# The causal mask of a block-sparse attention: from two TensorE matmuls a block to a VectorE add, with two query blocks sharing a pair of score banks

## The chip, the cores and the metric

The kernel runs on one core of a Trainium2 chip. The metric is the device time of one execution in microseconds. Lower is better. TensorE (PE) does the matmuls, VectorE (DVE), ScalarE (ACT) and GpSimd (POOL) the work on elements, and SyncE (SP) issues most transfers. Matmul results land in PSUM, which has eight banks of 512 fp32 values in each of 128 partitions; everything else lies in SBUF.

## The reference

Two decoder layers on a sequence of 512 tokens of width 1024. Each layer feeds three causal token mixers (a pooling, a short convolution, an attention) from one input projection, gates and adds their outputs, and then runs a gated feed-forward part. The change touches only the attention. It has 8 heads of 64 dimensions, and its sequence is cut into 2 blocks of 256 keys:

```python
gate = einsum('bhqd,bhnd->bhqn', q_i, kmean)        # queries against each block's mean key
gate = where(past, gate, NEG)                       # only blocks before the query's own
s_sel = where(valid, einsum(q_i, k_sel) * scale, NEG)
s_own = einsum('bhqd,bhkd->bhqk', q_i, k_own) * scale
s_own = where(kpos[None, :] <= qpos[:, None], s_own, NEG)    # the causal mask
p = softmax(concatenate([s_sel, s_own], axis=-1))
out = einsum(p_sel, v_sel) + einsum(p_own, v_own)
```

With two blocks only, the queries of the second block see the first block whole (the kernel has a penalty for the case in which the reference masks it) and their own block up to the diagonal.

## The kernel before

All activations lie transposed, features on the partitions. Every fp32 product is made of three matmuls on values split into a high part and a rest: high by high, high by rest, rest by high. The splits of the weights are made on the way: ScalarE copies the high part (`whi`, L327) and VectorE subtracts (`wlo`, L330). All matmuls go through one helper, L151, and all transposes through L157; both keep the program's order on TensorE. The order on the other engines is set by a scheduler when the program is built, except for instructions that are pinned.

**The order around the attention is written by hand.** The ordinary matmuls of the gates and of the branch projections run as the main line. Every 2,048 columns of main matmuls a *tick* happens. At a tick every *fiber* (a generator) that is due goes one step on; after that `run_bulk` adds `bulk_rate` to a credit and issues side tasks while the credit lasts. In layer 0 the side tasks of this stage are 16 long dot products of VectorE (L376, each of 1,024 elements, with a transfer of its own on the sync queue), which make two of the six modulation vectors. In layer 1 there are no side tasks in this stage. What is left of them is flushed after the attention projection (L954).

**The attention** (L661) is one fiber. For each of the 4 head pairs it makes the transposed queries and keys (`to_features`, four transposes each) and then starts four units, one for each block of 128 queries, with `GAP` = 2, 3, 3, 3 ticks between them. A unit (L580) has three steps:

1. It takes a pair of PSUM banks (`ps_pair`, of which two exist), one bank for each of the two heads. It writes the mask into the diagonal block of each bank by a matmul of a bf16 identity with a bf16 mask, and then accumulates six score matmuls on it, three for each head. A score matmul uses 64 rows of the array, since a head has 64 dimensions; the two heads use different rows. The score width is 256 columns for units 0 and 1, 384 for unit 2 and 512 for unit 3. VectorE then takes the maximum, ScalarE the exponentials with their sums, VectorE the reciprocal and the scaling (L598 to L623).
2. `WAIT` = 2, 3, 3, 3 ticks later TensorE transposes the probabilities (L157), ScalarE and VectorE split them (L634, L635).
3. Two ticks later TensorE multiplies them with the values (L644), and the result is put together and split (L649 to L654).

So unit 0's transposes fall on the tick at which unit 1 starts, unit 1's on the tick of unit 2, unit 2's on that of unit 3; unit 3's have a tick for themselves. Units 0 and 1 put the product of step 3 into a bank of its own, units 2 and 3 into the first of their score banks.

Of the kernel before, what the change touches and what calls it, by code (L numbers as in the profile page):

```python
# [12 lines left out]
F32 = mybir.dt.float32  # L13
F32R = mybir.dt.float32r
BF16 = mybir.dt.bfloat16
# [6 lines left out]
P = 128  # L22
# [5 lines left out]
HD = 64  # L28
PAIRS = HEADS // 2
TT = S // P  # L30
# [5 lines left out]
BLOCK = 256  # L36
# [43 lines left out]
def hybrid_trunk(ctx, tc, xT, ws, ada, cols, pool_w, qk_w, crow, pos, con, out):  # L80
    nc = tc.nc
    V, A, T = nc.vector, nc.scalar, nc.tensor

    const = ctx.enter_context(tc.tile_pool(name="const", bufs=1))
# [8 lines left out]
    def nm(s):  # L93
        uid[0] += 1
        return f"{s}{uid[0]}"

    def bigt(dt=F32R):
        return big.tile([P, S], dt, tag="big", name=nm("big"))

    def tmp():  # L100
        return work.tile([P, S], F32, tag="tmp", name=nm("tmp"), bufs=5)

    def ps_mm():
        return psum.tile([P, S], F32, tag="mm", name=nm("mm"), bufs=4)

    def ps_pair():
        return psum.tile([P, 2, S], F32, tag="pair", name=nm("pair"), bufs=2)

    def w4(shape, dt=F32):
        return work.tile(shape, dt, tag="w4", name=nm("w4"), bufs=6)  # L110

    def sm(shape, dt=F32, tag="sm", bufs=8):
        return small.tile(shape, dt, tag=tag, name=nm(tag), bufs=bufs)
# [8 lines left out]
    bulk_rate, credit = [0.0], [0.0]  # L122
# [27 lines left out]
    def matmul(*a, **k):  # L150
        tc.keep_in_program_order(T.matmul(*a, **k))  # L151
# [4 lines left out]
    def transpose(*a):  # L156
        tc.keep_in_program_order(T.transpose(*a))  # L157
# [38 lines left out]
    ident = const.tile([P, P], F32, name="ident")  # L196
    make_identity(nc, ident)
    ones = const.tile([P, P], F32, name="ones")
    nc.gpsimd.memset(ones, 1.0)
    ident16 = const.tile([P, P], BF16, name="ident16")  # L200
    nc.gpsimd.tensor_copy(ident16, ident)
    mask = const.tile([P, P], BF16, name="mask")
    nc.gpsimd.memset(mask, 0.0)
    nc.gpsimd.affine_select(out=mask, in_=mask, compare_op=ALU.is_ge, fill=NEG,
                            base=0, pattern=[[-1, P]], channel_multiplier=1)
# [207 lines left out]
    def ada_tasks(l, parts, early=False):  # L413
        out = []
        for part in parts:
            for j in range(KT):
                out.append((1.2, lambda part=part, j=j: ada_step(l, part, j, early)))
            out.append((0.2, lambda part=part: ada_end(l, part)))
        return out
# [157 lines left out]
    GAP = (2, 3, 3, 3)  # L577
    WAIT = (2, 3, 3, 3)

    def unit(hp, i, q, k, v, y, nrq, prq):  # L580

        w = P * (i + 1)
        wm = max(w, BLOCK)
        s = ps_pair()

        for a in range(2):
            matmul(s[:, a, i * P:w], ident16, mask, start=True, stop=True)
        for z, (qa, ka) in enumerate(((0, 0), (0, 1), (1, 0))):
            for a in range(2):
                r = slice(a * HD, (a + 1) * HD)  # L590
                matmul(s[:, a, :wm], q[qa][r, i * P:(i + 1) * P], k[ka][r, :wm],
                       start=False, stop=(z == 2), skip_group_check=True)
        cell = lambda: sm([P, 2], tag="asm", bufs=16)
        nsc, sc = nrq[:, i, 2 * hp:2 * hp + 2], prq[:, i, 2 * hp:2 * hp + 2]
        m, nb, den = cell(), cell(), cell()
        pr = [tmp() for _ in range(2)]
        if w <= BLOCK:
            V.tensor_reduce(m, s[:, :, :w], axis=AX.X, op=ALU.max)  # L598
            V.tensor_mul(nb, m, nsc)
            for a in range(2):  # L600
                A.activation(pr[a][:, :w], s[:, a, :w], AF.Exp, bias=nb[:, a:a + 1],
                             scale=sc[:, a:a + 1], accum_out=den[:, a:a + 1])
        else:

            gs, pen, mp, nbp, d2 = cell(), cell(), cell(), cell(), cell()
            V.tensor_reduce(gs, s[:, :, :BLOCK], axis=AX.X, op=ALU.add)
            V.tensor_mul(gs, gs, sc)
            V.tensor_scalar(pen, gs, NEG * BLOCK * SCALE, NEG, op0=ALU.is_lt, op1=ALU.mult)
            V.tensor_reduce(mp, s[:, :, :BLOCK], axis=AX.X, op=ALU.max)
            V.tensor_add(mp, mp, pen)  # L610
            V.tensor_reduce(m, s[:, :, BLOCK:w], axis=AX.X, op=ALU.max)
            V.tensor_max(m, m, mp)
            V.tensor_mul(nb, m, nsc)
            V.tensor_add(nbp, nb, pen)
            for a in range(2):
                A.activation(pr[a][:, :BLOCK], s[:, a, :BLOCK], AF.Exp, bias=nbp[:, a:a + 1],
                             scale=sc[:, a:a + 1], accum_out=den[:, a:a + 1])
                A.activation(pr[a][:, BLOCK:w], s[:, a, BLOCK:w], AF.Exp, bias=nb[:, a:a + 1],
                             scale=sc[:, a:a + 1], accum_out=d2[:, a:a + 1])
            V.tensor_add(den, den, d2)  # L620
        V.reciprocal(den, den)
        for a in range(2):
            V.tensor_scalar(pr[a][:, :w], pr[a][:, :w], den[:, a:a + 1], None, op0=ALU.mult)  # L623
        yield WAIT[i]

        pt = [None] * 2
        for aa in ([0, 1],) if i < 2 else ([0], [1]):
            n = len(aa)
            tp = ps_mm().rearrange("p (j a q) -> p j a q", a=n, q=P)[:, :i + 1]
            for a in aa:  # L630
                for j in range(i + 1):
                    transpose(tp[:, j, a - aa[0], :], pr[a][:, j * P:(j + 1) * P], ident)
            both = w4([P, i + 1, n, 2, P], F32R)
            A.activation(both[:, :, :, 0], tp, AF.Copy)  # L634
            V.tensor_sub(both[:, :, :, 1], tp, f32(both)[:, :, :, 0])  # L635
            for a in aa:
                pt[a] = both[:, :, a - aa[0]]
        yield 2


        po = (s[:, 0] if i >= 2 else ps_mm()).rearrange("p (a h q) -> p a h q", a=2, h=2)
        for a in range(2):
            for j in range(i + 1):
                matmul(po[:, a].rearrange("p h q -> p (h q)"), v[hp // 2][j][:, hp % 2 * 2 + a].rearrange("p h d -> p (h d)"),  # L644
                       pt[a][:, j].rearrange("p h q -> p (h q)"), start=(j == 0), stop=(j == i))
        c = slice(i * P, (i + 1) * P)
        t = tmp()
        part, total = t[:HD, :2 * P].rearrange("p (a q) -> p a q", a=2), t[:, 2 * P:3 * P]
        A.activation(part, po[HD:, :, 0], AF.Copy)  # L649
        V.tensor_add(part, part, po[:HD, :, 1])  # L650
        for a in range(2):
            V.tensor_add(total[a * HD:(a + 1) * HD], part[:, a], po[:HD, a, 0])
        A.activation(y[0][:, c], total, AF.Copy)
        V.tensor_sub(y[1][:, c], total, f32(y[0])[:, c])  # L654
# [6 lines left out]
    def attention(l, qk, v, nrq, prq, y_attn):  # L661

        for hp in range(PAIRS):
            q = to_features(l, qk, 0, hp)
            yield 1
            k = to_features(l, qk, 1, hp)
            y = bigt(), bigt()
            y_attn.append(y)
            yield 2
            for i in range(TT):  # L670
                start(unit(hp, i, q, k, v, y, nrq, prq))
                if i < TT - 1:
                    yield GAP[i]
            yield 1
# [45 lines left out]
    for l in range(L):  # L720
# [7 lines left out]
        for n, (k, lo, hi) in enumerate([(k, 0, S) for k in range(KT)] if l == 0 else HALVES + REST):  # L728
# [17 lines left out]
            w = held[k]  # L746
# [94 lines left out]
        for j in range(2):  # L841
# [8 lines left out]
            z = bigt(F32)  # L850
# [33 lines left out]
        for t in range(TT):  # L884
            for half in range(2):
                src = v_ps[t][:, half * BLOCK:(half + 1) * BLOCK].rearrange("p (n d) -> p n d", d=HD)
                o = v[half][t]
# [15 lines left out]

        if l == 0:
            bulk.extend(ada_tasks(l, (SC2, SH2), True))
        bulk_rate[0] = 0.35
        ahead_now[0] = 3

        def gate():
# [194 lines left out]
        for part, (along, single, pairs) in enumerate(PARTS):  # L1104
# [18 lines left out]
            for _ in range(single):  # L1123
                wg = next_w()
                g = ps_mm()
                feature_tile(g, wg)
                u = ps_mm()
# [5 lines left out]
            if l + 1 < L:  # L1133
                if part == 0:
                    later = ada_tasks(l + 1, (SC1, SH1, SC2, SH2))
                n = DOTS[part]
# [4 lines left out]
            if part + 1 < len(PARTS):  # L1141
                for n in range(KT):
                    if n == KT // 2:
                        bulk_rate[0] = 0.0
                    o = ps_mm()
# [117 lines left out]
```

## Time and profile before

| | us |
|---|---|
| time before, median of 3 runs | 1461.12 |
| lowest and highest of the 3 | 1460.99, 1461.18 |
| the profiled execution's own time | 1461.3 |
| its span in the profile | 1459.5 |
| TensorE matmuls busy | 1451.3 |
| VectorE busy | 1053.5 |
| ScalarE busy | 665.8 |
| GpSimd busy | 105.9 |

The profile is of one execution. The span goes from the first instruction to the last; the execution's own time has what lies around it too. TensorE's clock was granted in full throughout (1.00). Matmuls overlap in their pipeline, so the busy time of a group of matmuls is more than what it holds up; the distance from one matmul's start to the next one's is what it takes of TensorE's row. In the timeline, a row is "start us, us, engine line op out<-in xcount", and neighbouring instructions of one kind are merged.

### The profile page before, as it was taken

The page shows a single profiled execution, that of the slowest core. Times are in us where ns is not written, and L with a number is a line of the kernel's source. Part 1 is how long each engine was busy: PE and PEld are TensorE (multiplying, and loading weights), DVE is VectorE, ACT ScalarE, POOL GpSimd, SP SyncE. Part 2 cuts the span into 40 slices and gives each one's busy share as a digit, 9 for nine tenths or more (in the row PEclk, how much of TensorE's full clock was granted, in tenths as well). Part 3 has the DMA queues.
Part 4 walks back from the last instruction along what each step waited for, and adds up shares of the span by engine and source line. Part 5 has one row for each costly group of instructions (what it writes and reads, how often), then busy time and mean ns, then how long its engine had stood idle before and what let it go on. Part 6 is the DMA issues. An engine that isn't in the chain of part 4 may idle for free.

```text
span 1459.5 us, 21946 instructions
## 1 busy us (share of the span) xinstructions
PE 1451.3 (99%) x8443; PEld 1267.9 (87%) x8443; DVE 1053.5 (72%) x1855; ACT 665.8 (46%) x1138; POOL 105.9 (7%) x157
## 2 busy tenths in 40 slices
PE   9999999999999999999999999999999999999998
PEld 7888888788989998989988878788889889989997
DVE  7988888748686867677797766776587757657663
ACT  4634555443454452535444355555335525534450
POOL 0000000001100210211000000000020102111200
PEclk9999999999999999999999999999999999999999
DMA  9645334445336766756545422222462436637522
GB/s 351 219 142 173 121 110 138 137 159 152 109 114 205 201 174 202 188 146 203 191 146 176 161 77 73 73 77 98 158 194 78 138 122 165 183 98 192 137 85 84
DMA packets 84409, 217.19 MB, mean 149 GB/s; under 512 B 10832, under 2 KB 23760, under 8 KB 84304
## 3 DMA queue, kind: packets, MB, share of 16 engines
q1 hardware_dynamic: 67456, 177.37, 35.9%
q0 software_dynamic: 16128, 37.76, 11.8%
q8 instruction: 66, 1.08, 0.3%
q10 hardware_dynamic: 720, 0.66, 0.1%
q14 instruction: 39, 0.32, 0.1%
HBM read 213.65 MB, written 2.10 MB: 148 GB/s over the span
## 4 chain that ended last, share of the span: by engine, by line
PE 96%; DVE 2%; DMA 1%; ACT 1%; issue 0%; SPq 0%; ACTq 0%
PE mm L151 82%; PE pair L151 13%; PE mm L157 2%; DVE wlo L330 1%; DMA w<-in_ada 0%; DMA x<-in_xT 0%; DVE w L376 0%; ACT whi L327 0%; DVE tmp L485 0%; DVE big L504 0%; DVE big L488 0%; ACT big L487 0%; ACT big L491 0%; DVE tmp L476 0%; DVE big L477 0%
## 5 line engine op out<-in xcount | busy, mean ns | idle before, releaser
L151 PE MATMUL mm<-big,whi 128*128 128x512 f32 (+1 forms) x4362 | 1080.9, 339 | 1.5 <-DVE big L488 0.9
L151 PEld LDWEIGHTS mm<-big,whi 128*128 128x128 f32 x4362 | 745.6, 190 | 86.6 <-DVE big L488 1.7
L151 PE MATMUL mm<-big,wlo 128*128 128x512 f32 (+1 forms) x2181 | 735.9, 337 | 0.0
L151 PEld LDWEIGHTS mm<-big,wlo 128*128 128x128 f32 x2181 | 413.8, 190 | 44.4
L327 ACT ACTIVATE whi<-raw 128x1024 fp32r<-128x1024 f32 (+2 forms) x240 | 248.9, 1039 | 288.6 <-PE mm L151 205.0
L330 DVE TENSOR_TENSOR wlo<-raw,whi 128x1024 fp32r<-128x1024 f32 (+2 forms) x240 | 283.6, 1192 | 53.1 <-ACT whi L327 52.7
L327 ACT ACTIVATE whi<-w 128x1024 fp32r<-128x1024 f32 x72 | 76.2, 1058 | 146.0 <-PE mm L151 93.1
L958 DVE SCALAR_TENSOR_TENSOR x<-mm,mod,x 128x512 f32<-128x512 f32 (+1 forms) x90 | 61.8, 688 | 82.8 <-PE mm L151 82.7
L256 POOL DMA_DIRECT2D w<-in_ws x72 | 47.7, 672 | 968.1 <-DVE w L376 390.7
L330 DVE TENSOR_TENSOR wlo<-w,whi 128x1024 fp32r<-128x1024 f32 x72 | 86.7, 1220 | 30.8 <-ACT whi L327 30.1
L376 DVE SCALAR_TENSOR_TENSOR w<-w,csil 128x1024 f32<-128x1024 f32 x80 | 95.9, 1219 | 16.3 <-DMA w<-in_ada 16.2
L151 PE MATMUL pair<-whi,big 128*128 128x512 f32 x224 | 76.7, 390 | 0.0
L258 POOL DMA_DIRECT2D w<-in_ws x72 | 64.9, 934 | 147.8 <-DMA w<-in_ws 134.4
L151 PE MATMUL pair<-big,whi 128*128 128x256 f32 (+1 forms) x376 | 74.0, 294 | 0.0
L151 PEld LDWEIGHTS pair<-big,whi 128*128 128x128 f32 x376 | 60.4, 191 | 2.2
L151 PE MATMUL mm<-whi,big 128*128 128x512 f32 x160 | 57.3, 394 | 1.5 <-ACT big L501 1.2
L151 PE MATMUL pair<-big,wlo 128*128 128x256 f32 (+1 forms) x188 | 55.3, 294 | 0.0
L918 DVE SCALAR_TENSOR_TENSOR big<-big,mm 128x512 f32<-128x512 f32 x48 | 32.6, 683 | 26.4 <-PE mm L151 26.1
L151 PEld LDWEIGHTS pair<-whi,big 128*128 128x128 f32 x224 | 42.1, 188 | 8.6
L515 DVE TENSOR_TENSOR big<-tmp,big 128x512 fp32r<-128x512 f32 x48 | 33.0, 691 | 22.3 <-ACT big L514 21.3
L514 ACT ACTIVATE big<-tmp 128x512 fp32r<-128x512 f32 x48 | 29.7, 622 | 34.6 <-DVE tmp L1097 12.5
L151 PE MATMUL pair<-wlo,big 128*128 128x512 f32 x112 | 43.6, 390 | 0.0
(192 smaller groups left out, 1242.5 us busy)
## 6 DMA issues: line engine op xcount, KB each, us to landing
raw<-in_ws SPq DMA_DIRECT2D x146, 512.0 KB, 3.5
w<-in_ada SPq DMA_DIRECT2D x80, 512.0 KB, 5.2
w<-in_ws POOLq DMA_DIRECT2D x144, 256.0 KB, 4.6
raw<-in_ws SPq DMA_DIRECT2D x64, 256.0 KB, 3.8
raw<-in_ws SPq DMA_DIRECT2D x24, 384.0 KB, 3.3
raw<-in_ada SPq DMA_DIRECT2D x16, 512.0 KB, 3.3
raw<-in_ws SPq DMA_DIRECT2D x16, 448.0 KB, 5.6
raw<-in_ws SPq DMA_DIRECT2D x36, 128.0 KB, 2.9
```

What stands on the lines that cost most here:

```text
L151: tc.keep_in_program_order(T.matmul(*a, **k))
L157: tc.keep_in_program_order(T.transpose(*a))
L256: nc.gpsimd.dma_start(dst, self.source(0, 1))
L258: nc.gpsimd.dma_start(dst, self.source(*other), accum_op=ALU.add)
L327: A.activation(hi[:, :n], raw[:, :n], AF.Copy)
L330: ins = V.tensor_sub(lo[:, :n], raw[:, :n], f32(hi)[:, :n])
L376: return V.scalar_tensor_tensor(aw, aw, 1.0, csil, op0=ALU.mult, op1=ALU.mult, accum_out=mod[l][:, part, j:j + 1])
L514: A.activation(hi, src, AF.Copy)
L515: last_split[0] = V.tensor_sub(lo, src, f32(hi))
L918: V.scalar_tensor_tensor(sg, sg, 1.0, branch, op0=ALU.add, op1=ALU.mult)
L958: V.scalar_tensor_tensor(x[k][:, lo:hi], src, mod[l][:, part, k:k + 1], x[k][:, lo:hi], op0=ALU.mult, op1=ALU.add)
```

## The change

The mask matmuls go, and with them the bf16 identity. The mask is now an fp32 tile. When a unit's scores are done, VectorE adds the mask to the diagonal blocks in PSUM, in place: one add for both heads.

Units 0 and 1 of a head pair need 256 score columns each, which is half a bank. They now share one pair of banks, unit 0 in the first half and unit 1 in the second. Unit 0 issues the score matmuls of both, twelve in one stretch, and one VectorE add masks both (2 heads by 2 blocks by 128 elements). Unit 1 issues no matmul and no add at its start and goes on with its maximum; it still starts two ticks after unit 0. Units 2 and 3 have an add of their own (2 heads by 128 elements). So there are three adds in a head pair where there were eight mask matmuls, and three bank pairs are taken where there were four. The rate of side tasks in this stage goes from 0.35 to 0.27 credits a tick.

```diff
-    ident16 = const.tile([P, P], BF16, name="ident16")
-    nc.gpsimd.tensor_copy(ident16, ident)
-    mask = const.tile([P, P], BF16, name="mask")
+    mask = const.tile([P, P], F32, name="mask")
...
+    first_two = {}
+
     def unit(hp, i, q, k, v, y, nrq, prq):
 
         w = P * (i + 1)
-        wm = max(w, BLOCK)
-        s = ps_pair()
-
-        for a in range(2):
-            matmul(s[:, a, i * P:w], ident16, mask, start=True, stop=True)
-        for z, (qa, ka) in enumerate(((0, 0), (0, 1), (1, 0))):
-            for a in range(2):
-                r = slice(a * HD, (a + 1) * HD)
-                matmul(s[:, a, :wm], q[qa][r, i * P:(i + 1) * P], k[ka][r, :wm],
-                       start=False, stop=(z == 2), skip_group_check=True)
+
+        def scores(o, i, n):
+            for z, (qa, ka) in enumerate(((0, 0), (0, 1), (1, 0))):
+                for a in range(2):
+                    r = slice(a * HD, (a + 1) * HD)
+                    matmul(o[:, a], q[qa][r, i * P:(i + 1) * P], k[ka][r, :n], start=(z == 0), stop=(z == 2))
+
+        if i == 0:
+            s = first_two[hp] = ps_pair()
+            for u in range(2):
+                scores(s[:, :, u * BLOCK:(u + 1) * BLOCK], u, BLOCK)
+            diag = s.rearrange("p a (g c) -> p a g c", c=P)[:, :, 0:TT:TT - 1]
+            V.tensor_add(diag, diag, mask.unsqueeze(1).unsqueeze(1).to_broadcast([P, 2, 2, P]))
+        elif i == 1:
+            s = first_two.pop(hp)[:, :, BLOCK:]
+        else:
+            s = ps_pair()
+            scores(s[:, :, :w], i, w)
+            diag = s[:, :, i * P:w]
+            V.tensor_add(diag, diag, mask.unsqueeze(1).to_broadcast([P, 2, P]))
...
-        bulk_rate[0] = 0.35
+        bulk_rate[0] = 0.27
```

## The prediction

> **What bounds the kernel now.** I read the page first: the shares of the engines (part 1) and the chain that ended last (part 4); then the instructions grouped by shape; then what TensorE waited for.
>
> ```profile
> PE 1451.3 (99%) x8443; PEld 1267.9 (87%) x8443; DVE 1053.5 (72%) x1855; ACT 665.8 (46%) x1138; POOL 105.9 (7%) x157
> ...
> PE 96%; DVE 2%; DMA 1%; ACT 1%; issue 0%; SPq 0%; ACTq 0%
> ...
> L151 PE MATMUL pair<-mask,ident 128*128 128x128 bf16 x64 | 9.1, 224 | 0.0
> ...
> PE mm L151 <- ACT big L501: 1.2, 1, 1.2
> PE pair L151 <- POOL ones L199: 1.1, 1, 1.1
> PE mm L151 <- DVE big L488: 0.9, 4, 0.3
> ```
>
> TensorE is busy for 99% of the span and makes 96% of the chain. Its longest waits add up to a few microseconds, and none of these three is in the attention. So time is won here by taking work out of TensorE's own row, and lost when TensorE is made to wait. A busy total does not say what a matmul costs, because matmuls overlap: the 64 mask matmuls show 9.1 us busy. I therefore take prices from the distance between starts, in the timeline of TensorE around the attention units of the first head pair of layer 0.
>
> ```profile
> 134.29 0.62 PE L151 MATMUL mm<-big,whi 128*128 128x512 f32 x2
> 134.74 0.39 PE L151 MATMUL mm<-big,wlo 128*128 128x512 f32 x1
> 134.97 0.28 PE L151 MATMUL pair<-mask,ident 128*128 128x128 bf16 x2
> 135.19 0.62 PE L151 MATMUL pair<-big,big 64*128 64x256 f32 x6
> 135.74 0.74 PE L151 MATMUL mm<-big,whi 128*128 128x512 f32 x2
> ...
> 141.12 0.39 PE L151 MATMUL mm<-big,wlo 128*128 128x512 f32 x1
> 141.35 0.28 PE L151 MATMUL pair<-mask,ident 128*128 128x128 bf16 x2
> 141.57 0.62 PE L151 MATMUL pair<-big,big 64*128 64x256 f32 x6
> 142.12 0.44 PE L157 MATMUL mm<-ident,tmp 128*128 128x128 f32 x2
> ...
> 161.20 0.96 PE L151 MATMUL pair<-big,big 64*128 64x512 f32 x6
> 162.09 0.88 PE L157 MATMUL mm<-ident,tmp 128*128 128x128 f32 x6
> 162.72 0.48 PE L151 MATMUL mm<-big,whi 128*128 128x512 f32 x1
> ...
> 172.39 0.39 PE L151 MATMUL mm<-big,wlo 128*128 128x512 f32 x1
> 172.62 1.04 PE L157 MATMUL mm<-ident,tmp 128*128 128x128 f32 x8
> 173.41 0.71 PE L151 MATMUL mm<-big,whi 128*128 128x512 f32 x2
> ```
>
> The first group is unit 0, the second unit 1 with unit 0's transposes behind it, the third unit 3's scores with unit 2's transposes, the last unit 3's transposes, which follow an ordinary matmul directly. There are 4 units for each of 4 head pairs in each of 2 layers: 32 in all, two mask matmuls each.
>
> **The masks that go.** Two mask matmuls hold TensorE from 134.97 to 135.19, 0.22 us. An ordinary matmul of 512 columns is followed by the next after 0.225 us (134.29 to 134.74, two), that is 0.056 for 128 columns, so streaming two masks takes 0.11. The other 0.11 lies between the end of the stream and the start of the score matmuls, which use 64 rows instead of 128. That part is a change of the array's shape and I expect it to stay when an ordinary matmul comes ahead of the scores. So each of units 0, 2 and 3 saves 0.11 us. The ends: 0.22, if the remainder belongs to the masks; 0.055, if the change has to wait for the whole shown length of the last 512-column matmul (0.39, so 0.165 after its 0.225 slot). I take 0.11, since the wait after the mask is the only entry into a score group that the trace has.
>
> The Trainium skill (TensorEngine Tiling (Array Packing), section Tiling Modes, Key Properties) says that changing the tiling mode drains TensorE. That speaks against counting the full 0.22 for a mask; by the rule it is 0.11, and the trace agrees as far as its 0.11 of idle streaming between the last mask and the scores shows.
>
> **Unit 1 moved into unit 0's stretch.** From the last ordinary matmul ahead of it to the transposes behind it, unit 1 takes 141.12 to 142.12, 1.00 us. With masks and scores gone the transposes follow directly, as at 172.39 to 172.62: 0.23. That is 0.77 less. The six score matmuls now stand behind unit 0's six, in the same shape: 768 columns more for each head. Unit 3's group has just 768 columns more than unit 0's, and takes 0.89 (161.20 to 162.09) against 0.55 (135.19 to 135.74): 0.34 more. Net 0.43. The transposes gain a little too. Six behind a score group take 0.63 (162.09 to 162.72), so eight would take 0.84 at the same rate; eight behind an ordinary matmul take 0.79 (172.62 to 173.41): 0.05.
>
> Sum on TensorE for a head pair: 3 x 0.11 + 0.43 + 0.05 = 0.81; for 8 of them, 6.5 us. In the built program TensorE's order is otherwise the same; nothing else is removed or moved on it.
>
> **The adds that come.** VectorE gets three adds for a head pair: one of 512 elements (both blocks) and two of 256. The trace has no VectorE write into these banks. The nearest rows read them, with the same element counts, and write elsewhere:
>
> ```profile
> L1068 DVE TENSOR_TENSOR tmp<-tmp,pair x36: 411/418/425, 440.8 to 1409.6; 128x256 f32<-128x256 f32 x36
> L1023 DVE TENSOR_TENSOR tmp<-pair,tmp x4: 681/682/682, 426.6 to 1147.8; 128x512 f32<-128x512 f32 x4
> ...
> 134.90:177.00 42.10, 42.10 (x226) 33.70 (x224) 34.55 (x82) 22.80 (x50) 0.00 (x0) 1.00 0.48 163
> ...
> 894.90:937.60 42.70, 42.50 (x226) 34.03 (x224) 30.10 (x73) 21.91 (x51) 0.00 (x0) 1.00 0.22 75
> ...
> L376 DVE SCALAR_TENSOR_TENSOR raw<-raw,csil 128x1024 f32<-128x1024 f32 x16 | 19.3, 1218 | 0.5 <-DMA raw<-in_ada 0.5
> ```
>
> I take 0.68 + 2 x 0.42 = 1.52 us for a head pair (estimate; half or twice that are the ends). In the two stage rows the third busy figure is VectorE's: 34.55 of 42.10 us in the first head pair of layer 0, 30.10 of 42.70 in the second of layer 1. So 1.5 more fits: VectorE's throughput does not become the bound (it would need five times as much). In layer 0 the 16 long dots of the stage (19.3 us) are also spread thinner, 0.27 credits a step instead of 0.35, which spares it about a quarter of them (some 4 us by that row) in the stretch up to the transposes, against 6 us of adds in that layer. The moved dots cost TensorE nothing as long as they run beside it; each brings its load on the sync queue along, so the weight loads there change places with them. Nothing in the list of TensorE's waits names a weight load in this stage, so I give that no price. In layer 1 no dots stand in this stage and the rate changes nothing. The removed copy of the identity on GpSimd, before the first matmuls, I cost at nothing: the one wait for GpSimd, 1.1 us, is for the ones, which are set earlier.
>
> **What the adds make late.** An add stands between a unit's scores and its maximum, so the chain maximum, exponentials, reciprocal, scaling, transpose starts later. VectorE works in order: behind an add that waits for scores stand weight splits, output splits and dots, and TensorE would wait for those. What counts is the spare time until the transposes. Unit 0 of the first pair, VectorE and ScalarE:
>
> ```profile
> 136.04 1.22 DVE L376 SCALAR_TENSOR_TENSOR raw<-raw,csil 128x1024 f32<-128x1024 f32 x1
> ...
> 137.19 0.42 DVE L598 TENSOR_REDUCE asm<-pair 128x2 f32<-128x256 f32 x1
> 137.65 0.16 DVE L599 TENSOR_TENSOR asm<-asm,nrq 128x2 f32<-128x2 f32 x1
> 137.94 0.45 ACT L601 ACTIVATE tmp<-pair,asm,nrq 128x128 f32<-128x128 f32 x1
> ...
> 138.29 1.23 DVE L376 SCALAR_TENSOR_TENSOR raw<-raw,csil 128x1024 f32<-128x1024 f32 x1 [0.49 <-DMA raw<-in_ada]
> 138.72 0.21 ACT L601 ACTIVATION_READ_ACCUMULATOR tmp<-pair,asm,nrq 128x1 f32 x1
> ...
> 139.45 0.16 DVE L621 RECIPROCAL asm<-asm 128x2 f32<-128x2 f32 x1
> 139.64 0.48 DVE L623 TENSOR_SCALAR tmp<-tmp,asm 128x128 f32<-128x128 f32 x2
> ...
> 256.47 0.88 DVE L623 TENSOR_SCALAR tmp<-tmp,asm 128x512 f32<-128x512 f32 x2
> 257.12 1.04 PE L157 MATMUL mm<-ident,tmp 128*128 128x128 f32 x8
> ```
>
> The scaling ends at 140.12 and the transposes start at 142.12: 2.0 spare. After the change the add comes ahead of the maximum (0.68), and by the built order unit 1's maximum stands between unit 0's reciprocal and its scaling (0.42). A dot now stands between the maximum and the product; it waits for its load until 138.29 as before and ends at 139.45, so the product ends at about 139.6, the exponentials (1.1 us from the product's end at 137.81 to 138.93) at 140.7, the reciprocal at 140.9, the maximum at 141.3 and the scaling at 141.8. The transposes would start at 142.12 - 0.11 - 0.43 = 141.6. That is a wait of 0.2 to 0.3, once. In the other pairs of layer 0 the built order has no dot at that place.
>
> The last two rows are the tightest place, unit 3 of the third pair of layer 0: the second head's scaling ends at 257.35 while the transposes are already going. An add of 0.42 would make TensorE wait some 0.3 there; but the dot that now lies in that unit's chain (1.22) is elsewhere in the built order, so I charge nothing. Together: 0.3 us of new waiting. 6.5 - 0.3 = 6.2.
>
> **Forecast.** The profiled execution took 1461.3 us, with 1.8 around its span of 1459.5; the median is 1461.12, so nothing has to be rescaled. 1461.1 - 6.2 = 1454.9 us. Its own range: entry saving 0.055 instead of 0.11 gives 6.5 - 1.3 = 5.2 less 0.3, or 1456.2; adds twice as long, or a second wait of the first pair's kind in each layer, brings it to about 1456.6; no waiting and a part of the entry gone, 1453.6.
>
> **Rivals.**
> (a) The change of shape is free after an ordinary matmul: then each mask is worth 0.22, a pair 3 x 0.22 + 0.48 = 1.14, in all 9.1, and the time is 1452.0. For it: no row shows an entry without masks. Against it: the exit from a score group, in rows 135.19 to 135.74, also takes more than its 768 columns (0.34). Chance 0.10.
> (b) VectorE's queue becomes the bound of the attention, and it ends slower. Mechanism: an add reaches the head of the queue before its scores exist, the 1.22 us splits and dots behind it are held, and the scaling of units 2 and 3, which have little spare time, comes late. Place: the transposes of these two units. It decides from 0.81 us a head pair, where it eats the gain. If each pair loses one long operation at either unit, less some 0.5 of spare time each, that is 2 x 0.7 = 1.4 a pair, 11.5 in all, and the time is 1461.1 - 6.5 + 11.5 = 1466. For it: the 257.12 row, and VectorE at 34.55 of 42.10. Against it: no long operation is added, fewer dots, and unit 1's chain starts a whole interval earlier. Chance 0.08.
> (c) The same, half as bad: 0.5 to 0.8 us of waiting a pair, 1458.5 to 1461, no change that shows. Chance 0.08.
> (d) The stretch is not one stretch: in the built program the twelve score matmuls do stand together, so I give this no chance.
>
> **Numbers.** Forecast 0.74, (a) 0.10, (b) 0.08, (c) 0.08. A measurement of this kernel tells about 0.2% (2.9 us) from no change. Faster by more than that: forecast and (a), 0.84; within it 0.08; slower 0.08. The range reaches from rival (a), 1452.0, to 1458.2, and leaves out (b), (c) and what the forecast has beyond its ends.
>
> **What would show it.** Right: no mask row; score groups of twelve with 0.89 us to the next ordinary matmul; the last ordinary matmul to the scores 0.31 to 0.34 (0.225 if (a), 0.39 if the whole matmul is waited for); unit 0's transposes 0.23 behind an ordinary matmul; adds at 0.42 and 0.68; head pairs of some 41.3 us instead of 42.1 to 42.3. Wrong: waits of the transposes for the scaling (L623 now) above 0.8 us a head pair, or waits for weight splits in this stage.

## The result and the profile after

The changed kernel takes 1459.07 us (median of 21 runs, 1458.27 to 1460.27) against 1460.94 (21 runs) of the kernel before: ratio 0.9987, 95% interval 0.9982 to 0.9993. It is faster, by 1.9 us. The forecast was 6.2 us faster, 1454.9, with a range of 1452.0 to 1458.2. The time lies above the range.

First the page and the list of what TensorE waited for. The last line is the only new entry of size in that list. (One old entry grew from 0.3 to 1.2 us; it stands in the first 20 us, at the end of which the two kernels are 0.2 us apart.)

```profile
span 1456.9 us, 21848 instructions
...
PE 1444.2 (99%) x8379; PEld 1263.0 (87%) x8379; DVE 1063.1 (73%) x1879; ACT 664.0 (46%) x1138; POOL 105.7 (7%) x156
...
PE 91%; DVE 5%; ACT 2%; DMA 1%; issue 1%; SPq 0%; ACTq 0%
...
PE mm L157 <- DVE tmp L634: 3.6, 3, 1.7
```

TensorE's share of the chain fell from 96% to 91% and VectorE's rose from 2% to 5%: the end is now set in part by VectorE. L634 is the scaling of the probabilities, L157 their transposes: three waits, 3.6 us in all.

The places in TensorE's timeline for which the prediction gave numbers, first unit 0 with unit 1's scores, then unit 0's transposes, then the three waits:

```profile
134.85 0.39 PE L151 MATMUL mm<-big,wlo 128*128 128x512 f32 x1
135.17 0.97 PE L151 MATMUL pair<-big,big 64*128 64x256 f32 x12
136.07 0.74 PE L151 MATMUL mm<-big,whi 128*128 128x512 f32 x2
...
141.46 0.39 PE L151 MATMUL mm<-big,wlo 128*128 128x512 f32 x1
141.72 0.52 PE L157 MATMUL mm<-ident,tmp 128*128 128x128 f32 x2
142.00 0.71 PE L151 MATMUL mm<-big,whi 128*128 128x512 f32 x2
...
171.82 0.39 PE L151 MATMUL mm<-big,wlo 128*128 128x512 f32 x1
173.89 0.30 PE L157 MATMUL mm<-ident,tmp 128*128 128x128 f32 x1 [1.68 <-DVE tmp L634]
...
297.08 0.39 PE L151 MATMUL mm<-big,wlo 128*128 128x512 f32 x1
297.76 0.96 PE L157 MATMUL mm<-ident,tmp 128*128 128x128 f32 x7 [0.29 <-DVE tmp L634]
...
971.62 0.39 PE L151 MATMUL mm<-big,wlo 128*128 128x512 f32 x1
973.61 0.63 PE L157 MATMUL mm<-ident,tmp 128*128 128x128 f32 x4 [1.61 <-DVE tmp L634]
```

The last ordinary matmul to the scores: 0.32 us. The stretch of twelve: 0.90. Both are as forecast. But unit 3's transposes, which would stand 0.23 behind the ordinary matmul ahead of them, start 2.07, 0.68 and 1.99 behind it: 1.84, 0.45 and 1.76 us late, 4.05 in all.

The ordinary matmuls, transposes and value products are the same 8,187 instructions in both traces, in the same order, so their starts can be compared one by one. For each head pair the changed kernel is later by 0.227 us behind unit 0's stretch, and earlier by 0.76 at unit 1's place, 0.06 behind the transposes there, 0.126 at unit 2 and 0.126 at unit 3. That is 0.84 a pair and 6.7 for eight. Two places give a little less: unit 0's transposes of the first pair (0.17 us) and unit 2's of the third pair of layer 1 (0.10), where the scaling ends only just ahead of them. So TensorE's own row won what was expected, and 4.05 us were given back as waits at three of the 32 units. That leaves 2.65; the spans of the two profiled executions (1459.5 and 1456.9) differ by 2.6, with some tenths either way at other places, and the medians by 1.9.

### The profile page after: what moved, and what is told of

It is laid out like the page before. It is cut to its first block, busy times and chain, and to the rows that moved or that the text cites. A ratio compares the mean times of both kernels' runs of the same rounds, so it can differ in the third digit from the quotient of the medians.

```text
span 1456.9 us, 21848 instructions
## 1 busy us (share of the span) xinstructions
PE 1444.2 (99%) x8379; PEld 1263.0 (87%) x8379; DVE 1063.1 (73%) x1879; ACT 664.0 (46%) x1138; POOL 105.7 (7%) x156
## 4 chain that ended last, share of the span: by engine, by line
PE 91%; DVE 5%; ACT 2%; DMA 1%; issue 1%; SPq 0%; ACTq 0%
PE mm L151 78%; PE pair L151 12%; PE mm L157 2%; DVE wlo L328 1%; DVE raw L374 1%; DMA w<-in_ada 0%; DMA x<-in_xT 0%; ACT tmp L627 0%; ACT tmp L629 0%; ACT whi L325 0%; DVE w L374 0%; DMA raw<-in_ws 0%; DVE tmp L634 0%; DVE w L646 0%; DVE big L516 0%
```

## The experiments

Three theories see the loss in the late scaling; they differ in what makes it late. **Order**: in VectorE's queue, long operations (weight splits and dots of 1.2 us, gatings of 0.7) stand between the short steps of a unit's chain, and the queue that was built with the adds has more of them there. **Dots**: moving the dots by the lower rate does it. **Length**: the adds' own time does it. The kernel before was run again beside each group of experiments and took 1461.62 us beside the first four, 1461.39 beside the next four and 1461.36 beside the last two to be made (the old rate with the queueing, and the later tick); each ratio is against the one beside it.

**The rate alone, on the kernel before.**

```diff
-        bulk_rate[0] = 0.35
+        bulk_rate[0] = 0.27
```

> The kernel before with one change: the side-task rate 0.27 instead of 0.35. Three theories of where some 4 us of the expected 6.2 went, all of which see the loss in TensorE waiting for unit 3's scaled probabilities (171.8 and 297 us in layer 0, 971.6 us in layer 1). Order theory: VectorE's queue has long operations (weight splits and dots of 1.2 us, gatings of 0.7 us) between the nine short steps of a unit's chain, and the schedule that comes out with the adds puts more of them there. Dots theory: the moved dots alone do it. Length theory: the adds' own 0.43 and 0.69 us do it. Order and length theories: 1461 within 0.4 us here, no wait for scaled probabilities above 0.3 us. Dots theory: waits of some 2 us in layer 0, 1463.

Measured: 1461.53 us, ratio 1.0 (0.9992 to 1.0009), no wait for scaled probabilities. The rate by itself costs nothing: moved dots alone do not make the waits. (Its profiled execution took 1464.24, with one wait of 2.3 us in the feed-forward part; the other runs, at 1460.84 to 1462.09, do not show it in their time.)

**The changed kernel with the old rate.**

```diff
-        bulk_rate[0] = 0.27
+        bulk_rate[0] = 0.35
```

> The changed kernel with the rate back at 0.35. Dots theory: the two waits of layer 0 (1.8 and 0.45 us) go, the one of layer 1 stays: 1456.8. Order theory: another order in layer 0 with waits of about the same size, 1458 to 1460. Length theory: as the changed kernel, 1459, or worse by what the dots cost, up to 1460.

Measured: 1460.42 us, ratio 0.9991 (0.9982 to 0.9999). The waits are as large. The one of layer 1 stays where it was; those of layer 0 stand elsewhere, at unit 2 of the first pair (163.05 us) and at unit 3 of the second and third pairs (215.2 and 258.84):

```profile
PE mm L157 <- DVE tmp L634: 4.2, 4, 1.6
```

Four waits instead of three, with the same adds and the same work: another placing of the dots, another queue, other victims, as the order theory has it. The dots theory falls, since layer 0 still waits with the old rate. The time is 0.4 us above what the order and the length theory both allowed, so it does not tell these two apart.

**The adds left out.**

```diff
-            V.tensor_add(diag, diag, mask.unsqueeze(1).unsqueeze(1).to_broadcast([P, 2, 2, P]))
...
-            V.tensor_add(diag, diag, mask.unsqueeze(1).to_broadcast([P, 2, P]))
```

> The changed kernel without its VectorE adds: nothing is masked causally, the rest of the work is the same. Length theory: all waits go and the whole TensorE saving shows, 6.7 us: 1454.3. Order theory: a part of the waits can stay, since the long operations are still free to stand between the steps: 1454.3 to 1457. Dots theory: the waits of layer 0 stay: 1456.6.

Measured: 1456.71 us (1454.32 to 1457.65), ratio 0.9963 (0.9949 to 0.9977); the list of waits has no entry for the scaling. So the adds are needed for the waits. The time is above the 1454.3 that goes with no waits, but not because of the attention: see the table of the stages below. This alone cannot tell length from order, because the built queue changes with the adds: around unit 3 it is close to that of the kernel before (table below).

**The adds kept, splits and dots queued behind the chain** (`e4_hold` in the texts below). `split_w` and `ada_step` queue their VectorE instruction behind `hold` and `dots_after`, if these are set.

```diff
-            V.tensor_add(nbp, nb, pen)
+            hold[0] = dots_after[0] = V.tensor_add(nbp, nb, pen)
```

> The changed kernel with its adds, and with the weight splits and dots that are issued after unit 2 or 3 starts queued behind the last step of that unit's chain ahead of the exponentials. No work is taken away, the adds stay. Order theory: the waits for the scaled probabilities go: 1454.3 to 1455.5. Length theory: the waits stay for the most part: 1458 to 1459. Dots theory: the same as length theory, except that dots behind the chain help in layer 0: 1457.

Measured: 1454.87 us (1454.32 to 1455.36), ratio 0.9953 (0.9941 to 0.9966). No wait for the scaling is left, although every add is there. The length theory falls as a sufficient cause; the order theory stands. VectorE's row at the first of the three waits, unit 3 of the first pair, first in the kernel before:

```profile
165.55 0.68 DVE L918 SCALAR_TENSOR_TENSOR big<-big,mm 128x512 f32<-128x512 f32 x1
166.15 0.15 DVE L613 TENSOR_TENSOR asm<-asm,nrq 128x2 f32<-128x2 f32 x1
166.26 0.69 DVE L933 TENSOR_TENSOR big<-big,big 128x512 f32<-128x512 f32 x1
166.87 0.15 DVE L614 TENSOR_TENSOR asm<-asm,asm 128x2 f32<-128x2 f32 x1
166.94 1.22 DVE L330 TENSOR_TENSOR wlo<-raw,whi 128x1024 fp32r<-128x1024 f32 x1
...
171.17 0.87 DVE L623 TENSOR_SCALAR tmp<-tmp,asm 128x512 f32<-128x512 f32 x2
```

then in the changed kernel:

```profile
162.47 1.22 DVE L374 SCALAR_TENSOR_TENSOR raw<-raw,csil 128x1024 f32<-128x1024 f32 x1
...
163.61 0.43 DVE L603 TENSOR_TENSOR pair<-pair,mask 128x256 f32<-128x256 f32 x1
...
165.54 0.68 DVE L929 SCALAR_TENSOR_TENSOR big<-big,mm 128x512 f32<-128x512 f32 x1
...
167.48 0.68 DVE L944 TENSOR_TENSOR big<-big,big 128x512 f32<-128x512 f32 x1
168.08 0.15 DVE L623 TENSOR_TENSOR asm<-asm,asm 128x2 f32<-128x2 f32 x1
168.15 1.21 DVE L328 TENSOR_TENSOR wlo<-raw,whi 128x1024 fp32r<-128x1024 f32 x1
169.28 0.15 DVE L624 TENSOR_TENSOR asm<-asm,nrq 128x2 f32<-128x2 f32 x1
169.35 0.74 DVE L516 SCALAR_TENSOR_TENSOR big<-mm,colt,big 128x512 fp32r<-128x512 f32 x1
170.02 0.15 DVE L625 TENSOR_TENSOR asm<-asm,asm 128x2 f32<-128x2 f32 x1
...
172.53 0.16 DVE L631 TENSOR_TENSOR asm<-asm,asm 128x2 f32<-128x2 f32 x1 [1.70 <-ACT tmp L629]
```

and then with the queueing:

```profile
163.18 0.42 DVE L603 TENSOR_TENSOR pair<-pair,mask 128x256 f32<-128x256 f32 x1
...
167.17 0.15 DVE L623 TENSOR_TENSOR asm<-asm,asm 128x2 f32<-128x2 f32 x1
167.24 0.74 DVE L516 SCALAR_TENSOR_TENSOR big<-mm,colt,big 128x512 fp32r<-128x512 f32 x1
167.90 0.15 DVE L624 TENSOR_TENSOR asm<-asm,nrq 128x2 f32<-128x2 f32 x1
167.97 0.68 DVE L944 TENSOR_TENSOR big<-big,big 128x512 f32<-128x512 f32 x1
168.57 0.15 DVE L625 TENSOR_TENSOR asm<-asm,asm 128x2 f32<-128x2 f32 x1
168.64 1.22 DVE L328 TENSOR_TENSOR wlo<-raw,whi 128x1024 fp32r<-128x1024 f32 x1
171.09 0.16 DVE L631 TENSOR_TENSOR asm<-asm,asm 128x2 f32<-128x2 f32 x1 [1.22 <-ACT tmp L629]
```

In the kernel before, the weight split (166.94) stands behind the last step ahead of the exponentials (L614). In the changed kernel a weight split (168.15) and the split of the next pair's transposed queries or keys (169.35) stand between the last three short steps of 0.15 us; L623 ends at 168.23 and L625, on which the exponentials wait, at 170.17. With the queueing the weight split comes after L625, which ends at 168.72; two shorter operations (167.24 and 167.97) still stand between. At the third wait a weight split stands behind the exponentials too: they end at 971.70 and the step that needs them starts at 972.28.

Over the eight units 3, from 0.31 us after the start of the last score matmul to the end of the last step ahead of the exponentials, with the operations above 0.6 us that do not belong to the chain and start in between:

| kernel | chain, mean us | longest | long operations in the 8 chains | their time, us |
|---|---|---|---|---|
| before | 4.88 | 5.96 | 9 | 8.3 |
| changed | 6.37 | 8.65 | 19 | 17.5 |
| adds left out | 4.99 | 6.49 | 10 | 9.0 |
| adds, queued splits and dots | 5.15 | 6.91 | 9 | 6.3 |

Of the 1.5 us by which the chain grew, 0.43 is the add itself, and about 1.1 is what came between: 9.2 us more of long operations over 8 chains, 1.15 a chain. As an estimate from these numbers, the three waits of 1.84, 0.45 and 1.76 us without 0.43 each would still be 2.8 of 4.05.

**The same queueing on the kernel before.** The edit is that of the run above.

> The kernel before, masks by matmul, with the splits and dots queued behind the chains of units 2 and 3 as in e4_hold. Order theory: there was next to nothing to wait for before, so nothing to win: 1461 within 0.5 us. Length theory: the same. Rival: the queueing is worth 4 us by itself, whatever the mask does: 1457.

Measured: 1461.0 us, ratio 1.0 (0.9991 to 1.0009). The queueing wins nothing by itself, so what it wins in the changed kernel is the waits that came with the change.

**The weight splits alone queued.**

```diff
-            V.tensor_add(nbp, nb, pen)
+            hold[0] = V.tensor_add(nbp, nb, pen)
```

> e4_hold with the weight splits alone queued behind the chains, the dots free as in the changed kernel. Order theory: the splits make the larger part in both layers, layer 1 has no dots at all; the wait at 971.6 us goes wholly, of those in layer 0 (2.3 us) up to half stays: 1455 to 1456. If it were the dots: 1457.

Measured: 1455.7 us (1454.21 to 1456.72), ratio 0.9962 (0.995 to 0.9975), no wait for the scaling. Not to be told from 1454.87 with the dots queued as well. Holding the splits is enough. It does not price splits and dots apart in layer 0, though: both are pinned to the program's order, so a dot issued after a held split waits with it, and VectorE's whole order differs from that of the run before by the place of one dot. In layer 1 there are no dots, and there the splits alone did it.

**Queued splits and dots with the old rate**: `bulk_rate[0] = 0.35` in the kernel with the queueing.

> e4_hold with the side-task rate back at 0.35. If the rate matters only through the order of VectorE's queue, it does nothing once splits and dots stand behind the chains: 1454.9 within 0.6 us. If the thinner dots are needed to make room for the adds: 1456 or more, with waits in layer 0 alone.

Measured: 1455.43 us (1454.32 to 1457.02), ratio 0.996 (0.9946 to 0.9974), no wait for the scaling. The lower rate is not needed to make room.

**Adds alone, no sharing of banks**, with the queueing.

```diff
+        wm = max(w, BLOCK)
+        s = ps_pair()
+        scores(s[:, :, :wm], i, wm)
+        diag = s[:, :, i * P:w]
+        V.tensor_add(diag, diag, mask.unsqueeze(1).to_broadcast([P, 2, P]))
```

> Adds instead of mask matmuls, but every unit keeps a bank pair and a start of its own, as before; four adds a head pair; splits and dots queued behind the chains as in e4_hold. From the starts in the changed kernel each of 32 units should save 0.126 us: 4.0, no waits: 1457.0. Length theory: waits come back, since the adds stay: 1459 to 1461. If the merge were what wins, the saving would be near zero.

Measured: 1457.79 us, ratio 0.9978 (0.9969 to 0.9987), 3.6 us. By the starts each of the 32 units comes 0.126 us earlier, 4.0 in all, as expected.

**Sharing alone, masks by matmul**, rate 0.35. Four mask matmuls and twelve score matmuls stand in one stretch; only the first mask of a bank opens it.

```diff
+            for j, (lo, u, n) in enumerate(parts):
+                for a in range(2):
+                    matmul(s[:, a, lo + u * P:lo + (u + 1) * P], ident16, mask, start=(j == 0), stop=True,
+                           skip_group_check=(j > 0))
```

> The other part alone: mask matmuls stay, units 0 and 1 share a bank pair and their scores and masks stand in one stretch; no adds; rate 0.35. From the starts: unit 1's place saves 0.76 + 0.06 a head pair, unit 0's grows by 0.35 for scores and 0.13 for masks: 0.34 x 8 = 2.7, so 1458.3 if no wait comes. Order theory: without adds the order stays near that of the kernel before, waits under 1 us: 1458 to 1459.3. Length theory: 1458.3.

Measured: 1458.18 us, ratio 0.998 (0.9971 to 0.9989), 3.2 us. By the starts unit 0 grows by 0.46 and unit 1's place gives 0.82 back: 0.35 a pair, 2.8 in all. This half brings no VectorE work, and the scaling is never waited for. By the medians it wins more than the whole change (3.2 us against 1.9), but the intervals overlap.

**More time instead of another order.**

```diff
-    WAIT = (2, 3, 3, 3)
+    WAIT = (2, 3, 3, 4)
```

> The changed kernel with its own order, but unit 3's transposes and its product one tick later (WAIT 2, 3, 3, 4). They get some 2.5 us more time, more than the longest wait of 1.8 us. Order and length theories alike: the waits of unit 3 go (3.6 us with the one at 297 us), 1454.9 to 1456; unit 3's transposes then stand behind the next pair's scores, within 0.1 us a pair. If the loss were not the lateness of unit 3's scaling: 1458 to 1460.

Measured: 1454.08 us (1453.0 to 1454.99), ratio 0.9949 (0.9936 to 0.9961). The order stays bad, but unit 3's transposes come a tick later and no longer meet it. This is the fastest kernel here, one number away from the change; against the queueing (0.9953) the intervals overlap.

**The two attention stages alone.** In their first 100 us the profiled executions differ from that of the kernel before by -0.2 to 1.1 us, ahead of any attention. The starts of the same TensorE instructions, compared from 100 to 330 us (layer 0) and from 800 to 1,030 us (layer 1) of the kernel before, leave that out. Each row is one execution, and up to 0.5 us of it comes from two places of layer 1 (843.7 and 935.4 us) at which the kernel before loses 0.3 and 0.2 us and some of the others do not:

| kernel | earlier in both stages, us |
|---|---|
| before, rate 0.27 | 0.3 |
| before, queueing | 0.1 |
| changed | 2.8 |
| changed, rate 0.35 | 1.4 |
| adds left out | 6.6 |
| adds, queued splits and dots | 6.9 |
| adds, queued splits alone | 6.8 |
| the same with rate 0.35, splits and dots queued | 6.9 |
| adds alone, queueing | 4.3 |
| sharing alone | 3.1 |
| unit 3 one tick later | 7.3 |

So with the adds left out the whole saving of 6.7 us does show in the attention, and so it does with the adds kept and the splits queued.

## Why the prediction was wrong

- **What bounds the kernel.** Right: TensorE's row. Taking 64 matmuls out of it moved everything behind it, unit by unit.
- **The masks.** 0.11 us for each of units 0, 2 and 3 was forecast; the adds-alone run gives 0.126. Of the 0.22 that two masks held, 0.09 stayed as the change to 64 rows: 0.32 from ordinary matmul to scores, against a slot of 0.227. Rival (a), the free change, is refuted. The Trainium skill (TensorEngine Tiling (Array Packing), section Tiling Modes) says that a change of the tiling mode drains TensorE. These rows agree with it, with 0.09 us.
- **Unit 1 in unit 0's stretch.** 0.43 net and 0.05 were forecast; 0.76 + 0.06 less 0.35 (0.227 and the 0.126 of unit 0's own masks) is 0.47. The TensorE sum, 6.5, came out at 6.7.
- **The adds.** 0.68 and 0.42 were forecast; the row of the 16 small ones gives 0.426, that of the 8 large ones 0.694:

```profile
L603 DVE TENSOR_TENSOR pair<-pair,mask x16: 418/426/433, 152.9 to 1005.1; 128x256 f32<-128x256 f32 x16
L596 DVE TENSOR_TENSOR pair<-pair,mask x8: 691/694/700, 137.3 to 978.4; 128x512 f32<-128x512 f32 x8
```

- **Unit 0 of the first pair.** Forecast: scaling ready at 141.8 and transposes wanted at 141.6. The second head's scaling ends at 141.86, the first head's at 141.67, and the transposes start at 141.72, 0.03 behind their slot of 0.23; with the transposes behind the first, this place loses 0.17 us against the other pairs, where 0.2 to 0.3 was forecast. Worked through step by step along the built queue, the chain came out right.
- **Unit 3: the step that failed.** I charged 0.3 us of new waiting in all, and nothing at unit 3; at unit 3 alone it was 4.05. I followed the built queue at two places and took the rest as unchanged apart from the adds. Of the tightest place, unit 3 of the third pair in layer 0, I said that it would not wait, since the dot had left its chain; that held. But the first pair of layer 0 and the third of layer 1 waited 1.8 us each. In the kernel before they had about 1 us to spare (the first head's scaling ready at 171.65 for transposes at 172.62, and at 974.52 for 975.47). Two long operations and none started in their chains before, six and four after. The fourth pair of layer 0 had 2.5 us to spare (296.05 for 298.51) and still waited 0.45: none before, two after. These changes can be seen in the built order without a run; I did not go through all 16 units 2 and 3.
- **Rival (b)** named the place (the transposes of units 2 and 3, splits of 1.2 us), and the waits came there, at unit 3 alone. It had the price of one meeting too low (0.7 us for 1.84, 0.45 and 1.76) and wanted two in every pair; there were three in all. Its sum has a slip as well: eight times 1.4 is 11.2, not 11.5. Its mechanism, an add that holds the queue until its scores exist, is not what made the waits: at these three places the add starts 2.10, 1.29 and 0.74 us after the point 0.31 us behind the start of the last score matmul, and VectorE does not stand idle ahead of it. (It does ahead of seven other adds, 7.2 us in all, six of them in layer 1, and none of the three waits is there.) What spoke against it, "no long operation is added", missed the point: none is added to the kernel, but ten more came to start inside unit 3's chains.
- **Rival (c)**, 0.5 to 0.8 us a pair and 1458.5 to 1461, is where the result fell: 0.5 us a pair on average (4.05 over eight), 1459.07. It should have had more than 0.08, since spare times of 0.2 to 1 us stood in the trace. Its mechanism was that of (b), so its number came true through another one.

Not settled is why the schedule puts more long operations into unit 3's chain with the adds. That it does is in the built order and in the table; no run here shows what in the scheduler does it.

## What to carry to other kernels

When a step is put into a dependent chain on an in-order engine, price the whole queue, not the step: list for every instance of the chain what stands between its steps in the new order, and set it against the spare time of that instance. A chain of nine short steps leaves a gap for a long operation at every joint. The spare time of the old kernel alone does not name the victim: here the tightest instance (0.2 us) did not wait, and one with 2.5 us did. Where a late instance is found, a tick more for its consumer, or a place for the chain ahead of the long operations, won the loss back here.

## What the runs showed of the hardware

A TensorE change from 128 to 64 rows costs about 0.09 us going in: 0.318 us between starts against 0.227 in the ordinary row. It is the same whether a 512-column fp32 matmul or a 128-column bf16 one precedes: the entry from the mask was 0.149 for a stream of 0.057 (a quarter of 0.227). The other bank pair does not cost it, since a mask matmul, which uses 128 rows and writes the same banks as the scores, started 0.230 after an ordinary one.

A VectorE add in place on PSUM took within 2% of what operations of the same size took that read these banks and write SBUF (0.694 against 0.682 for 512 elements, 0.426 against 0.418 for 256).
